# Two-level Strassen MLP: eight weight splits move from the first superblock to the second, and the piece loads of matmul2 keep the program's order

## The chip, the cores and the metric

The kernel runs on one core of a Trainium2 chip. The metric is the device time of one execution in microseconds, as a median over runs. Weights and activations come in as float32 and the result goes out as float32; all matrix products take float16 operands and accumulate in float32.

## The reference

```
x: [8, 1024, 1024]   w1: [1024, 4096]   w2: [4096, 1024]     (float32)
h = x @ w1
h = 0.5 * h * (1 + tanh(sqrt(2 / pi) * (h + 0.044715 * h ** 3)))
out = h @ w2
```

## The kernel before

The 8192 rows of x are taken in eight superblocks of 1024 rows (sb 0 to 7). For each, a first stage computes g = gelu(x @ w1) for all 4096 hidden columns and leaves it in SBUF as four tiles g11, g12, g21 and g22 (two halves of rows by two halves of hidden columns); a second stage computes g @ w2 and stores it.

**Products.** Both stages use a Strassen form: a 2 by 2 block product in seven products, numbered 1 to 7, instead of eight. Products 1, 2 and 3 have a raw block of the weight as operand (block 11, 21, 22), and 5, 6, 7 and 4 have a sum of blocks, which DVE makes. In superblocks 0 and 1 this is done once (one level). From superblock 2 on each of w2's seven operands is itself cut in four quarters, and seven second-level products are taken of it. The second-level operands are again three raw quarters and four sums (5, 6, 7, 4, the tuple `SUMS`). matmul1_late does likewise for part of w1's products, with sums that are called s1, s5, s2, s7 and s3.

**Stages and what they leave in DRAM.** Superblocks 0 and 1 run `matmul1` and `matmul2_made`. While TensorE works there, the operands of the later superblocks are made once and stored in DRAM: w1's in `w1_d`, w2's first-level operands and raw blocks in `w2_d`, and the second-level sums of each w2 operand m in `in_d[m]`. One such second-level sum is called a split here: job `pmn` makes sum n of operand m. It is `make` in `split_jobs`: a buffer, two DVE tensor_tensor instructions, and a 512 KB store issued by POOL (L979). Raw quarters need no split; they are read from `w2_d`.

From superblock 2 on `matmul1_late` and `matmul2` run. matmul1_late works through `PAIR`, an order of small pieces written out by hand, for eight pairs of chunks (`Pair`). Its weights come as eight half-quads, one for each pair (class `StoredHalf`, L284): each loads six pieces of 512 KB, one for each entry of `GROUPS`: operands (1, 5); the sums s1, s5 (in a buffer "mu"); then (2, s2), (7, s7), (3, s3) and (6, 4). The sums s1, s5 of half-quads 1 and 2 are loaded, and those of later ones are made on POOL from operands 1 and 5 (L315, keys k2 to k7 of `PAIR`). Half-quads 0 and 1 of the next superblock are created inside matmul2, when products 7 and 3 begin, and their later pieces are placed in the parts of the g tiles that matmul2 no longer reads (`ROOM`).

matmul2 takes the seven first-level products in the order 4, 1, 2, 5, 6, 7, 3. Each is an object of class `Inner`; `load` fetches its seven second-level pieces on SP's queue, sums from `in_d` (L1034) and raw quarters from `w2_d` (`load_raw`, L1038). The pieces of a product are loaded when the product before it begins, so while product 7 runs, product 3's are asked for. All go in buffers "u", but for the last two steps of product 3: raw quarter 3 goes to a "mu" and sum 4 to the "xi" buffer. Product 4 is begun early: its seven pieces are asked for at the end of matmul1_late.

**Order of jobs in superblocks 0 and 1.** The table `FILL[sb]` gives each slot its jobs. A slot `mq` follows product m's quarter q of the rows; sixteen matmuls of 128x512 make one slot, so it takes 3.46 us of TensorE. The products go 1, 2, 5, 6, 3, 7, 4. Jobs: `g` sums of g, `w` first-level w2 sums, `p` splits, `x` sums of the next x, `q` and `i` sums of w1's next quad and inner sums of x or w1.

**Order of loads.** SP issues nearly all loads. Instructions that go through `load_in_order` (L162) or `tc.keep_in_program_order` keep the order of the program among each other; a plain `nc.sync.dma_start` may be moved by the scheduler that runs when the program is built. In the program as built, SP issues product 3's raw quarter 3 (mu) and sum 4 (xi), and the next superblock's piece (s1, s5) of half-quad 1 (mu), at the end of matmul1_late, ahead of the rest of product 4's pieces.

**Buffers.** Pool `up` has 24 buffers "u" of 512 KB, `mp` 2 "mu", `xip` 1 "xi", `gcp` 4 "gc", `tp` 9 temporaries, and all eight PSUM banks are in use ("ps").

**Engines.** TensorE (PE) multiplies; L497 holds the products of matmul1 and the undivided half products, L712 the second-level parts in matmul1_late, L1082 second-level products in matmul2, L1124 the one-level products of matmul2_made. DVE makes sums (all at L138, helper `tt`) and combines PSUM results; ACT copies (L165) and applies the gelu (L510); POOL makes the inner sums of L315, some adds (L764) and issues the stores to out (L838 and others), the split stores (L979) and the casts of the next x rows (`x_cast`, 256 KB each). SP issues loads and the transposing loads of x (`x_transpose`).

Of the kernel before, what the change touches and what calls it, by code (L numbers as in the profile page):

```python
# [9 lines left out]
DT = mybir.dt.float16  # L10
# [4 lines left out]
P = 128  # L15
# [8 lines left out]
SUMS = tuple(W_SUM)  # L24
# [16 lines left out]
def slots(table):  # L41
# [4 lines left out]
    slots("""10:g60 p15;11:g61 p16;12:g62 p17;13:g63  # L46
    ;20:g50 w50 w51;21:g51 w52;22:w53 g52;23:g53 p14
    ;50:w60 w61;51:w62 w63;52:g30 g31;53:g32 g33
    ;60:w70 p25;61:w71 p26;62:w72 p27;63:w73 p24
    ;30:p35 w40;31:p36 w41;32:p37 w42;33:p34 w43;73:x5;40:x7 x6;41:x3 q5;42:q6 q7 q4  # L50
    ;43:i2 i7 i3 i1 i5""".replace("\n    ", "")),
    slots("""10:g60 w50;11:g61 w51;12:g62 w52;13:g63 w53
    ;20:g50 p55;21:g51 p56;22:g52 p57;23:g53 p54
    ;50:w60 w61;51:w62 w63;52:g30 g31;53:g32 g33
    ;60:p65 w70;61:p66 w71;62:p67 w72;63:p64 w73
    ;30:w40 w41;31:w42 w43;32:p75;33:p76
    ;70:p77 p74;71:x5 p45;72:x7 p46;73:x6 p47
    ;40:p44;41:x3;42:i2;43:i3""".replace("\n    ", "")),
)


# [11 lines left out]
def kernel(  # L73
# [7 lines left out]
    nc = tc.nc  # L81
# [10 lines left out]
    NI = I // P // 2  # L92
    OH = O // 2
# [10 lines left out]
    mp = ctx.enter_context(tc.tile_pool(name="mp", bufs=2))  # L104
# [15 lines left out]
    in_d = {m: dram.tile([P, 4, NI // 2, OH // 2], DT, name=f"in_d{m}") for m in range(1, 8)}  # L120
    w2_d = {
        (k, m): dram.tile([P, 2, 2, HALF], DT, name=f"w2_d{k}_{m}")
        for k in range(2)
        for m in tuple(W_TERM) + SUMS + ("12",)
    }
# [8 lines left out]
    def unit(rows, cols):  # L134
        return up.tile([P, rows, cols], DT, name="u")

    def tt(out, in0, in1, op, pin=False):
        i = nc.vector.tensor_tensor(out=out, in0=in0, in1=in1, op=op)  # L138
        if pin:
            tc.keep_in_program_order(i)  # L140
# [12 lines left out]
    def chunks(t):  # L153
        return t.rearrange("p o (c n) -> p o c n", c=QC)
# [6 lines left out]
    def load_in_order(out, in_, **kw):  # L161
        return tc.keep_in_program_order(nc.sync.dma_start(out=out, in_=in_, **kw))  # L162
# [26 lines left out]
    class MadeQuad:  # L189
# [10 lines left out]
        def load(self):  # L200

            for b, t in self.raw.items():
                k0 = (int(b[0]) - 1) * KH
                halves = t.rearrange("p (h k) n -> p k h n", h=2)
                for k in range(0, KH, 2):
                    cast_in(
                        halves[:, k:k + 2],
                        w1v[int(b[1]) - 1, :, k0 + k:k0 + k + 2, self.q * QW:(self.q + 1) * QW],
                        pool_copy,
                        view=lambda st: st.rearrange("p k (h n) -> p k h n", h=2),  # L210
                    )
# [753 lines left out]
    def split_jobs(m, pieces):  # L965
        t = {}

        def operand(v, h):
            if isinstance(v, int):
                return t[v][:, h * QC:(h + 1) * QC, :]  # L970
            k, b = int(v[0]) - 1, int(v[1]) - 1
            return chunks(pieces()[2 * k + h])[:, b]

        def make(n):
            u, op, v = W_SUM[n]
            t[n] = (mp.tile([P, NI // 2, OH // 2], DT, name="mu") if n in (7, 4) else unit(NI // 2, OH // 2))
            for h in range(2):
                tt(t[n][:, h * QC:(h + 1) * QC, :], operand(u, h), operand(v, h), op, True)
            nc.gpsimd.dma_start(out=in_d[m][:, SUMS.index(n)], in_=t[n])  # L979

        return [lambda n=n: make(n) for n in SUMS]
# [35 lines left out]
    class Inner:  # L1017
# [7 lines left out]
        def load(self, steps=STEPS):  # L1025
            for j in steps:
                if j in self.y:
                    continue
                pool, name = {(3, 3): (mp, "mu"), (3, 4): (xip, "xi")}.get((self.m, j), (up, "u"))
                self.y[j] = pool.tile([P, NI // 2, OH // 2], DT, name=name)  # L1030
                if j in W_TERM:
                    self.load_raw(j)
                else:
                    nc.sync.dma_start(out=self.y[j], in_=in_d[self.m][:, SUMS.index(j)])  # L1034

        def load_raw(self, j):
            k, b = (int(d) - 1 for d in W_TERM[j])
            nc.sync.dma_start(  # L1038
                out=self.y[j].rearrange("p c n -> p (c n)"),
                in_=w2_d[k, self.m][:, b].rearrange("p h n -> p (h n)"),  # L1040
            )

        def make(self, j):
# [219 lines left out]
```

## Time and profile before

| | |
|---|---|
| runs | 1459.35, 1467.58, 1461.14 us |
| median | 1461.14 us |
| profiled execution: its own time | 1462.57 us |
| profiled execution: span | 1460.8 us |
| PE (matmul) | 1450.4 us busy, 99% of the span |
| DVE | 1211.2 us, 83% |
| ACT | 681.1 us, 47% |
| POOL | 620.8 us, 42% |
| granted TensorE clock | 1.0 |
| DMA | 472.72 MB, mean 324 GB/s |
| median of a load u from w_d (SP), issue to landing | 10.2 us (512 KB) |
| median of a load u from in_d (SP) | 10.3 us |
| median of a store out_dram from u (POOL) | 11.1 us |

The profile is that of one execution. Busy time is what an engine worked; its idle time before an instruction is put down to the releaser that came last. In a line of a group or of the timeline, `u<-w_d` is output and input by the program's names, w_d standing for w1_d or w2_d; `x10` is a run of ten instructions; `[1.87 <-DMA u<-w_d]` is 1.87 us of idle time before it, ended by that DMA. Landing is the time from a DMA's issue to its end. Times are microseconds from the start of the span.

### The profile page before, as it was taken

Reading aid. Unit: us, or ns where it says so; the run is one execution under the profiler, and the core shown is the slowest. Engines: PE = TensorE matmul, PEld = TensorE weight load, DVE = VectorE, ACT = ScalarE, POOL = GpSimd, SP = SyncE. Lnnn points to the kernel's source line nnn. Section 1 sums busy time; section 2 is a strip of 40 time slices with the busy share of each in tenths; the row PEclk is TensorE's granted clock in tenths of the full one; section 3 lists DMA queues with packets and bytes.
Section 4 is the critical chain, followed back from the end, with each engine's and each line's share of the span. In section 5 each row is a group of like instructions: output and inputs, shape, how many; then the busy total and the mean of one; then the engine's idle time right before and its main releaser. Section 6 shows DMA issues by size and latency. Waiting matters only on the chain.

```text
span 1460.8 us, 28718 instructions
## 1 busy us (share of the span) xinstructions
PE 1450.4 (99%) x10635; PEld 1039.4 (71%) x10635; DVE 1211.2 (83%) x2029; ACT 681.1 (47%) x1406; POOL 620.8 (42%) x634
## 2 busy tenths in 40 slices
PE   9999999999999999999999999999999999999998
PEld 5444444444467888778877788777887778877887
DVE  5657659748768899889998899988998889988897
ACT  5665116641068611784118831388214872168610
POOL 1442222213359411792128820488005961168411
PEclk9999999999999999999999999999999999999999
DMA  9999999798799999999999999999999989996597
GB/s 322 339 348 383 290 331 358 276 304 259 296 359 272 282 352 366 373 264 337 338 377 370 229 371 336 363 356 225 398 344 362 331 237 389 354 385 231 210 362 265
DMA packets 205709, 472.72 MB, mean 324 GB/s; under 512 B 75648, under 2 KB 80768, under 8 KB 204672
## 3 DMA queue, kind: packets, MB, share of 16 engines
q1 hardware_dynamic: 177632, 373.35, 74.1%
q0 software_dynamic: 27936, 97.53, 22.3%
q8 instruction: 83, 1.36, 0.4%
q14 instruction: 58, 0.48, 0.1%
HBM read 370.15 MB, written 115.34 MB: 332 GB/s over the span
## 4 chain that ended last, share of the span: by engine, by line
PE 87%; DMA 7%; issue 3%; POOL 1%; ACT 0%; SPq 0%; DVE 0%; POOLq 0%; DVEq 0%
PE ps L1082 35%; PE ps L712 23%; PE ps L497 21%; PE ps L1124 7%; DMA gc<-in_w_dram 3%; DMA u<-in_w_dram 2%; DMA w_d<-u 1%; PE ps L430 1%; DMA xb<-in_x_dram 1%; DMA u<-in_d 1%; POOL u L168 0%; POOL out_dram L826 0%; PE ps L407 0%; POOL in_d L979 0%; ACT u L165 0%
## 5 line engine op out<-in xcount | busy, mean ns | idle before, releaser
L165 ACT COPY tmp<-ps 128x512 f32<-128x512 f32 (+1 forms) x536 | 268.8, 540 | 313.3 <-PE ps L497 168.2
L497 PE MATMUL ps<-u 128*128 128x512 f16 x1552 | 363.7, 379 | 3.5 <-DMA u<-w_d 2.7
L1082 PE MATMUL ps<-u,gc 128*128 128x256 f16 x2592 | 290.0, 273 | 0.1
L1082 PEld LDWEIGHTS <-gc 128*128 128x128 f16 x2688 | 263.0, 98 | 30.7 <-issue 0.3
L138 DVE TENSOR_TENSOR tmp<-tmp,ps 128x256 f32<-128x256 f32 (+1 forms) x372 | 199.9, 545 | 87.0 <-PE ps L712 29.8
L497 PEld LDWEIGHTS <-u 128*128 128x128 f16 x1552 | 151.7, 98 | 150.6 <-DMA u<-w_d 3.6
L838 POOL DMA_DIRECT2D out_dram<-u x70 | 63.8, 949 | 443.7 <-DVE u L138 220.3
L712 PEld LDWEIGHTS <-u 128*128 128x128 f16 x2026 | 198.2, 98 | 55.4
L138 DVE TENSOR_TENSOR u<-u 128x2048 f16<-128x2048 f16 (+3 forms) x264 | 204.7, 814 | 33.1 <-DMA w_d<-u 12.6
L165 ACT COPY u<-ps 128x512 f32<-128x512 f32 (+1 forms) x134 | 78.0, 587 | 327.6 <-PE ps L1082 319.3
L1082 PE MATMUL ps<-u,g 128*128 128x256 f16 x1920 | 219.4, 273 | 0.0
L712 PE MATMUL ps<-u 128*128 128x256 f16 x1342 | 216.9, 273 | 0.0
L1082 PEld LDWEIGHTS <-g 128*128 128x128 f16 x2016 | 197.3, 98 | 22.8
L510 ACT ACTIVATE g<-tmp 128x512 f16<-128x512 f32 x282 | 174.0, 640 | 52.2 <-DVE tmp L138 51.2
L138 DVE TENSOR_TENSOR ps<-tmp,ps 128x256 f32<-128x256 f32 x444 | 181.3, 426 | 19.4 <-PE ps L712 12.2
L138 DVE TENSOR_TENSOR u<-u,ps 128x512 f32<-128x512 f32 x216 | 147.2, 683 | 25.9 <-PE ps L1082 16.7
L1124 PE MATMUL ps<-u,g 128*128 128x512 f16 x768 | 166.4, 379 | 0.0
L510 ACT ACTIVATE g<-ps 128x512 f16<-128x512 f32 x230 | 137.8, 600 | 24.8 <-PE ps L712 14.6
L1124 PEld LDWEIGHTS <-g 128*128 128x128 f16 x768 | 75.1, 98 | 90.7
L138 DVE TENSOR_TENSOR tmp<-ps,tmp 128x512 f32<-128x512 f32 x126 | 86.7, 690 | 54.2 <-PE ps L497 42.8
L764 POOL TENSOR_TENSOR tmp<-tmp 128x512 f32<-128x512 f32 x96 | 122.0, 1274 | 20.2 <-DVE tmp L138 13.4
L138 DVE TENSOR_TENSOR gc<-g,gc 128x2048 f16<-128x2048 f16 x78 | 95.1, 1219 | 1.3 <-PE ps L1082 1.3
(70 smaller groups left out, 1506.4 us busy)
## 6 DMA issues: line engine op xcount, KB each, us to landing
u<-w_d SPq DMA_DIRECT2D x347, 512.0 KB, 10.2
u<-in_d SPq DMA_DIRECT2D x162, 512.0 KB, 10.3
out_dram<-u POOLq DMA_DIRECT2D x70, 512.0 KB, 11.1
gc<-in_w_dram SPq DMA_DIRECT2D x48, 512.0 KB, 6.0
g<-w_d SPq DMA_DIRECT2D x45, 512.0 KB, 13.2
w_d<-u POOLq DMA_DIRECT2D x40, 512.0 KB, 7.1
w_d<-u SPq DMA_DIRECT2D x32, 512.0 KB, 8.9
xb<-in_x_dram POOLq DMA_DIRECT2D x56, 256.0 KB, 7.5
```

What stands on the lines that cost most here:

```text
L138: i = nc.vector.tensor_tensor(out=out, in0=in0, in1=in1, op=op)
L165: tc.keep_in_program_order(nc.scalar.copy(out=out, in_=in_))
L430: tc.keep_in_program_order(nc.tensor.matmul(bank[:, cols], lhsT=w[:, k, :], rhs=self.xs.blocks[f"{a}{r}"][:, k, cols], start=r == 1 and k ...
L497: tc.keep_in_program_order(nc.tensor.matmul(bank, lhsT=w, rhs=x, start=first and k == 0, stop=k == n - 1, skip_group_check=not first,))
L510: gelu_last[0] = nc.scalar.activation(out=out, in_=src, func=GELU, scale=scale)
L712: tc.keep_in_program_order(nc.tensor.matmul(out, lhsT=w, rhs=x, start=first and k == 0, stop=k == 1, skip_group_check=not first,))
L764: tc.keep_in_program_order(nc.gpsimd.tensor_tensor(out=t, in0=t, in1=temp("p", m), op=ADD))
L838: return nc.gpsimd.dma_start(out=rows, in_=src, **kw)
L1082: tc.keep_in_program_order(nc.tensor.matmul(bank[:, i * OH // 2:(i + 1) * OH // 2], lhsT=t[:, c, i * P:(i + 1) * P], rhs=self.y[j][:, c, : ...
L1124: tc.keep_in_program_order(nc.tensor.matmul(pair(bank), lhsT=a[:, c, :], rhs=chunks(pieces[c // QC])[:, :, c % QC, :], start=(first and c ...
```

## The change

Eight splits, those of w2's operands 2 and 3 (its raw blocks 21 and 22: p25, p26, p27, p24, p35, p36, p37, p34), leave the slots 60 to 33 of the first superblock's table and enter slots 52 to 41 of the second's. In the first superblock the sums w71 to w73 and w40 to w43 then stand in earlier slots. The moved splits 7 and 4 take "u" buffers instead of "mu". The loads of class `Inner` (L1034 and L1038) go through `load_in_order`. In the program as built, the orders of PE and ACT are as before; on DVE and POOL only the eight splits, their stores and the sums w7n and w4n stand elsewhere. On SP's queue product 3's last two pieces now follow its other five, and the piece (s1, s5) of the next superblock's half-quad 1 follows the first three pieces that go into g22.

```diff
--- before.py
+++ after.py
@@ -46,16 +46,16 @@
     slots("""10:g60 p15;11:g61 p16;12:g62 p17;13:g63
     ;20:g50 w50 w51;21:g51 w52;22:w53 g52;23:g53 p14
     ;50:w60 w61;51:w62 w63;52:g30 g31;53:g32 g33
-    ;60:w70 p25;61:w71 p26;62:w72 p27;63:w73 p24
-    ;30:p35 w40;31:p36 w41;32:p37 w42;33:p34 w43;73:x5;40:x7 x6;41:x3 q5;42:q6 q7 q4
+    ;60:w70 w71;61:w72 w73;62:w40 w41;63:w42 w43
+    ;73:x5;40:x7 x6;41:x3 q5;42:q6 q7 q4
     ;43:i2 i7 i3 i1 i5""".replace("\n    ", "")),
     slots("""10:g60 w50;11:g61 w51;12:g62 w52;13:g63 w53
     ;20:g50 p55;21:g51 p56;22:g52 p57;23:g53 p54
-    ;50:w60 w61;51:w62 w63;52:g30 g31;53:g32 g33
-    ;60:p65 w70;61:p66 w71;62:p67 w72;63:p64 w73
-    ;30:w40 w41;31:w42 w43;32:p75;33:p76
+    ;50:w60 w61;51:w62 w63;52:g30 g31 p25;53:g32 g33 p26
+    ;60:p65 w70 p27;61:p66 w71 p24;62:p67 w72;63:p64 w73
+    ;30:w40 w41;31:w42 w43;32:p75 p35;33:p76 p36
     ;70:p77 p74;71:x5 p45;72:x7 p46;73:x6 p47
-    ;40:p44;41:x3;42:i2;43:i3""".replace("\n    ", "")),
+    ;40:p44 p37;41:x3 p34;42:i2;43:i3""".replace("\n    ", "")),
 )
 
 
@@ -973,7 +973,7 @@
 
         def make(n):
             u, op, v = W_SUM[n]
-            t[n] = (mp.tile([P, NI // 2, OH // 2], DT, name="mu") if n in (7, 4) else unit(NI // 2, OH // 2))
+            t[n] = (mp.tile([P, NI // 2, OH // 2], DT, name="mu") if n in (7, 4) and m not in (2, 3) else unit(NI // 2, OH // 2))
             for h in range(2):
                 tt(t[n][:, h * QC:(h + 1) * QC, :], operand(u, h), operand(v, h), op, True)
             nc.gpsimd.dma_start(out=in_d[m][:, SUMS.index(n)], in_=t[n])
@@ -1031,13 +1031,13 @@
                 if j in W_TERM:
                     self.load_raw(j)
                 else:
-                    nc.sync.dma_start(out=self.y[j], in_=in_d[self.m][:, SUMS.index(j)])
+                    load_in_order(self.y[j], in_d[self.m][:, SUMS.index(j)])
 
         def load_raw(self, j):
             k, b = (int(d) - 1 for d in W_TERM[j])
-            nc.sync.dma_start(
-                out=self.y[j].rearrange("p c n -> p (c n)"),
-                in_=w2_d[k, self.m][:, b].rearrange("p h n -> p (h n)"),
+            load_in_order(
+                self.y[j].rearrange("p c n -> p (c n)"),
+                w2_d[k, self.m][:, b].rearrange("p h n -> p (h n)"),
             )
 
         def make(self, j):
```

## The prediction

> **What bounds the kernel now.** I read the page first, then TensorE's waits, the chain, and around the two places that the change touches the timelines and single DMAs. TensorE is busy throughout:
>
> ```profile
> PE 1450.4 (99%) x10635; PEld 1039.4 (71%) x10635; DVE 1211.2 (83%) x2029; ACT 681.1 (47%) x1406; POOL 620.8 (42%) x634
> ```
>
> The longest of its waits, in all:
>
> ```profile
> PE ps L497 <- DMA u<-w_d: 2.7, 2, 1.9
> ```
>
> So 1460.8 - 1450.4 = 10.4 us of the span are idle PE, the start-up included; only a wait that shows in PE's own idle time can be won back. The chain shows how tight the later superblocks are (start, length, what):
>
> ```profile
> 581.80 2.59 PE ps L497 x12
> ...
> 756.74 2.59 PE ps L497 x12
> ```
>
> That piece opens matmul1_late. It starts at 406.86, 581.80, 756.74, 931.71, 1106.65 and 1281.88: 174.95 us each, but 175.23 for the fifth, which lost 0.28 where product 4's first loads arrived (a chain piece of DMA u<-in_d at 1193.14). All other loss in reach lies between the first two superblocks, in the timeline (idle time before and releaser in brackets):
>
> ```profile
> 201.04 31.97 SPq L198 DMA_DIRECT2D u<-w_d  x10
> ...
> 211.33 1.90 PE L497 MATMUL ps<-u 128*128 128x512 f16 x8 [1.87 <-DMA u<-w_d]
> ...
> 214.02 10.53 PE L497 MATMUL ps<-u 128*128 128x512 f16 x48 [0.79 <-DMA u<-w_d]
> ...
> 225.40 9.87 PE L497 MATMUL ps<-u 128*128 128x512 f16 x45 [0.84 <-DVE tmp L138]
> ```
>
> 1.87 + 0.79 + 0.84 = 3.5 us. SP issues the second superblock's w1 quad only at 201.04, behind 16 transposing loads that ran from 167.92 to 197.34 while eight split stores and x stores shared the DMA engines.
>
> **Part 1, splits leave the first superblock.** Eight splits (p25 to p34) go. Each is two DVE instructions (1.29 us the pair), one POOL issue (0.54) and a 512 KB store: 10.3 us of DVE, which waited there anyway, and 4 MB of stores between 168 and 195. In the changed program's order the quad's four buffers come from sums of product 5 and from staging tiles, free long before, no longer from split tiles that wait for their stores. In later superblocks a transposing load takes 1.25 us of SP, so 16 take 20, not 29.4; the quad's loads start some 9 us earlier, against 3.5 of stall. I take the whole 3.5 as gained (bounds 0 and 3.5).
>
> **Part 2, splits enter the second superblock.** The same 10.3 us of DVE. p25 to p24 stand before 368.98, where DVE sat idle 9.62 us: hidden, with some 4 us left. p35 to p34 add 5.2 us from 376 on; gaps of 1.6, 1.5 and 6.1 us (until 409.98) take them. The new tile of a split may wait for an earlier split's store (4 to 10 us to landing there); behind it on DVE stand x3 and the inner sums. x3 is read by PE at 413.17 and was ready at 398.45; the inner sum of product 2 is read at 409.50 and was ready at 399.91, so 9.6 us of cover. Of POOL's eight issues and stores, those of p37 and p34 stand after the last store of a mu tile. Cost 0; if the cover is gone, up to 3 us (a rival below).
>
> **Part 3, the pinned loads.** The old order hoists three loads per superblock, product 3's last two (mu, xi) and the next superblock's mu (sums s1, s5 of half-quad 1), to the end of matmul1_late, some 90 us before use:
>
> ```profile
> 655.74 2.22 SPq L1038 DMA_DIRECT2D mu<-w_d  x1
> ...
> 663.70 0.49 SPq L284 DMA_DIRECT2D mu<-w_d  x1
> 667.92 0.32 SPq L1034 DMA_DIRECT2D xi<-in_d  x1
> ```
>
> They delay product 4's loads by three landings of 1.28 us, and xi's wait for its buffer (to 667.92) holds the queue. Those loads land 0.04 to 2.9 us before use; the new order gives them 4 us more. Since PE barely waited there, that wins 0.28 us in all.
>
> In the new order mu and xi follow product 3's other loads, and the third comes after three g loads: all three stand in the stretch where matmul2 ends. There the DMA engines are full, and POOL's stores of products 7 and 3 share them:
>
> ```profile
> L838 POOL DMA_DIRECT2D out_dram<-u x6: 725/794/1227, 745.8 to 757.8; - x6
> ...
> DMA to landing us min/median/max: 10.8/14.8/16.7
> ```
>
> While stores are queued, SP's loads land every 2.5 us (754.21, 756.83, 759.59, 762.14, 764.64, 767.12, 769.62, then 774.10 with two x casts between); before and after it is 1.28 (775.96, 777.17, 778.47). SP's own issue does not limit this: it issues when the load eight before has landed. Watch the sixth DMA behind the first three g loads, half-quad 1's (6,4) operand, issued at 746.97, with those behind it:
>
> ```profile
> 746.97 0.32 SPq L284 DMA_DIRECT2D u<-w_d  x1
> 755.02 0.32 SPq L284 DMA_DIRECT2D mu<-w_d  x1
> 755.38 19.05 SPq L284 DMA_DIRECT2D u<-w_d  x10
> ```
>
> Its own landing (min, median, max of this one DMA), and its first reader:
>
> ```profile
> DMA to landing us min/median/max: 17.7/17.7/17.7
> ```
> ```profile
> 771.98 1.03 PE L497 MATMUL ps<-u 128*128 128x512 f16 x4
> ```
>
> It lands at 764.64 and is read at 771.98: 7.3 us of cover. With three more loads ahead and the stores unchanged it gets the landing of the DMA three places behind, issued at 755.86, 18.2 us to landing: 774.10. PE would wait 774.10 - 771.98 = 2.1 us. The same reading at the five ends of a matmul2 that has a successor:
>
> - end at 581.80: read 597.03, new landing 599.55, wait 2.5
> - 756.74: 771.98, 774.10, 2.1
> - 931.71: 946.95, 949.18, 2.2
> - 1106.65: 1121.89, 1125.31, 3.4
> - 1281.88: 1297.12, 1297.65, 0.5
>
> Sum 10.7 us. The other loads of the stretch keep a little cover in this shift (product 3's own mu and xi 1.3 to 3.4 and 0.3 to 3.6 us; g loads down to -0.3), and those after 1121.89 gain what PE has already waited. Bounds: one landing of 1.28 either way at each place gives 5 to 17. The lower end at no sharing is a rival.
>
> The row that decides is the landing every 2.5 us beside stores. [...]
>
> **Sum** against the profiled execution (1462.57, span 1460.8): 1462.57 - 3.5 - 0.3 + 10.7 = 1469.5, +0.47%. The median of the runs shown (1461.14) is 1.4 below that execution; +0.47% on it is 1468.
>
> **Rivals.**
>
> *Gain alone.* The three loads cost 3 x 1.28 = 3.8 us of DMA time, less than the 4.6 to 7.3 us of cover at the (6,4) operand. If they displace stores rather than loads, nothing waits and 3.8 is won: 1461.14 - 3.8 = 1457.3. For it: no wait of PE there now. Against: the 2.5 us spacing holds at all five ends, whether five or eight loads are outstanding.
>
> *POOL's chain on top, slower.* POOL's first sum of half-quad 3 (L315) starts at 779.87, 0.16 after its load landed at 779.71. Behind it on POOL stands the second add of L764, for which a Gelu on ACT waits; that Gelu ran 1.36 us after the add, and the bank freed behind it was reused 0.94 us later: 2.3 us of cover. Three places on, the load lands at 785.90, 6.2 later; less 2.1 that PE already lost and 2.3 of cover, 1.8 more per end. About 2 us at five ends: 1468 + 10 = 1478. It decides once that load is over 4.4 us late. Against it: 3.6 of the 6.2 are two x casts, started by POOL behind PE's own progress, so they move back too; then it is near 3.8.
>
> *The clock.* The granted clock is 1.0 in all 40 slices, and idle times up to 1.87 did not lower it; the first seven matmuls took 3.17 us, 0.45 each against 0.216 later. A wait of 3.4 us, longer than any in this trace, could bring that back: ten matmuls at 0.23 more are 2.3 us per end, at one to four ends 1470 to 1477. [...]
>
> *Second superblock.* SP's order now has two mu loads behind each other at 400.65, the second waiting for the last mu store (landed 402.35, later by what DVE adds). If that holds half-quad 1's loads (cover 7.3 to 11.5 us) over 7 us, some 3 us are added: 1471.
>
> **How the numbers follow.** Forecast 0.52, its own range 1462 to 1474; gain alone 0.20; POOL's chain 0.13; clock 0.07; second superblock 0.08. 0.5% (7.3 us) is about what a measurement of this kernel can tell from no change. More than 7.3 won is out of reach, since 3.8 is all there is: 0.03, out of gain alone, for the runs' scatter. The forecast stands at the edge: 0.24 of it slower, the rest same. Slower: 0.24 + 0.13 + 0.06 + 0.06 = 0.49; same 0.48. Range: from gain alone (1457) to POOL's chain (1478), with 2 us at each end since the two medians scatter: 1455 to 1480.
>
> **What would show it.** Right: no idle PE near 201 to 226; PE waits of 2 to 3 us on DMA u<-w_d about 15 us after each matmul1_late starts, and periods near 177; product 4's loads landing 4 us or more ahead. Wrong: periods still 174.95 (gain alone); waits on ACT or POOL near 24 us (POOL's chain); matmuls 0.43 us apart (clock); PE idle between 407 and 430 (second superblock); or the 3.5 us at 211 still there.

## The result and the profile after

The changed kernel takes 1476.43 us (median of six runs, 1472.05 to 1478.50) against 1460.99 us for the kernel before (six runs). The ratio is 1.0101, with a 95% interval of 1.0081 to 1.0121: it is slower by about 15 us. The profiled execution took 1477.74 us with a span of 1476.0.

The page's line for TensorE, and then the list of its waits (total, times, longest):

```profile
PE 1454.5 (99%) x10635; PEld 1038.6 (70%) x10635; DVE 1210.7 (82%) x2029; ACT 680.9 (46%) x1406; POOL 620.0 (42%) x634
```
```profile
PE ps L497 <- DMA u<-w_d: 6.5, 3, 3.3
PE ps L497 <- ACT tmp L165: 5.5, 2, 2.8
```

Idle PE has grown from 10.4 us to 1476.0 - 1454.5 = 21.5. That is 11.1 of the 15.2 us by which the span grew; the other 4.1 are *busy* PE. The waits on DMA were there before (2.7 us), though not in these places; those on ACT are new.

Both kernels issue the same 10635 matmuls in the same order. So the start of each matmul in one trace can be set against the same matmul in the other, and what the difference grows by in a stretch is what that stretch cost. An end is the stretch where a matmul2 gives way to the next matmul1_late; the five are numbered in order of time. The (6,4) operand is that of half-quad 1, the load that the prediction follows. In us against the profiled execution before:

| stretch | after | of it PE's wait at the (6,4) operand or a g load | wait behind POOL | half-rate clock |
|---|---|---|---|---|
| start-up, to 30 us | -0.72 | | | |
| first to second superblock, 200 to 235 | -4.01 | | | |
| second superblock to 560 | +0.37 | 0.36 | | |
| end 1 (start 581.80 before) | +4.60 | 0 | 2.93 | 1.66 |
| end 2 (756.74) | +5.63 | 1.04 | 2.95 | 1.66 |
| end 3 (931.71) | +5.16 | 3.26 | 0 | 1.70 |
| end 4 (1106.65) | +3.44 | 3.43 | 0 | 0 |
| near 1201 | -0.29 | | | |
| end 5 (1281.88) | +1.00 | 0.99 | 0 | 0 |

The sum is +15.2, the whole growth of the span. The rest of end 3 is a step of 0.21 ahead of its wait. The start-up's 0.7 has nothing to do with the change: all later kernels but two show -0.7 to -1.0 there against this one execution.

The gain is where it was looked for. SP issues the second superblock's w1 quad at 193.75 us, 7.3 us earlier than before (some 9 were forecast). In the timeline the second superblock now begins without a wait, where before three pieces stood with 1.87, 0.79 and 0.84 us of idle time:

```profile
206.63 2.11 PE L1124 MATMUL ps<-u,g 128*128 128x512 f16 x9
208.57 14.62 PE L497 MATMUL ps<-u 128*128 128x512 f16 x67
```

The loss at end 2 shows all three mechanisms. SP's queue issues the (6,4) operand at 751.57, the answer on that one DMA gives 21.6 us to landing (17.7 before), and the matmul that reads it starts when it lands, at 773.25:

```profile
751.57 0.32 SPq L284 DMA_DIRECT2D u<-w_d  x1
```
```profile
DMA to landing us min/median/max: 21.6/21.6/21.6
```
```profile
773.25 1.04 PE L497 MATMUL ps<-u 128*128 128x512 f16 x4 [0.88 <-ACT g L510]
```

(751.57 + 21.6 = 773.2. The trace names ACT as releaser, but the 0.05 us between landing and start says that it is the load.) Some 12 us on, POOL's sum of half-quad 3 (L315) waits for its load, and the add of L764 stands behind it. An ACT copy out of PSUM waits for that add: it writes a temporary (`tmp<-ps`), so it needs a free buffer and not the add's result; by the code the add is the last reader of one. The PE waits for the bank that the copy empties. POOL before, and then POOL, ACT and PE after:

```profile
777.97 1.28 POOL L764 TENSOR_TENSOR tmp<-tmp 128x512 f32<-128x512 f32 x1
779.87 1.15 POOL L315 TENSOR_TENSOR mu<-u 128x512 f16<-128x512 f16 x1 [0.62 <-PE ps L712]
780.98 1.27 POOL L764 TENSOR_TENSOR tmp<-tmp 128x512 f32<-128x512 f32 x1
```

```profile
779.26 1.28 POOL L764 TENSOR_TENSOR tmp<-tmp 128x512 f32<-128x512 f32 x1
785.77 1.15 POOL L315 TENSOR_TENSOR mu<-u 128x512 f16<-128x512 f16 x1 [5.23 <-DMA u<-w_d]
786.88 1.26 POOL L764 TENSOR_TENSOR tmp<-tmp 128x512 f32<-128x512 f32 x1
```
```profile
788.18 0.59 ACT L165 COPY tmp<-ps 128x512 f32<-128x512 f32 x1 [4.37 <-POOL tmp L764]
```
```profile
788.81 1.04 PE L497 MATMUL ps<-u 128*128 128x512 f16 x4 [2.78 <-ACT tmp L165]
```

Then come 4 us in which the PE is busy and does half its work. The windows view (window, its length, busy time and instructions of PE, PEld, DVE, ACT and POOL, granted clock, DMA share, GB/s) for the wait and for what follows it:

```profile
785.50:788.80 3.30, 0.54 (x5) 0.33 (x4) 0.01 (x1) 0.62 (x2) 3.03 (x3) 1.00 1.03 423
788.80:792.90 4.10, 4.09 (x16) 2.03 (x16) 2.72 (x6) 3.58 (x7) 4.10 (x4) 0.61 1.02 415
```

At end 1 a window inside such a spell reads 0.50 (in the last section). At that rate a granted clock of 0.61 over 4.1 us is half rate for 3.2 us; over a 5.1 us window it reads 0.67 at ends 1, 2 and 3 alike, 3.4 us at half rate, so 1.7 us of work lost each time. Three such spells cost 5.0 us. That busy PE grew by 4.1 only is because other stretches had less of it, the start-up above all (25.40 us for its 185 matmuls, 27.23 before).

### The profile page after: what moved, and what is told of

It reads as the page before. It is cut to its first block, busy times and chain, and to the rows that moved or that the text cites. A ratio compares the mean times of both kernels' runs of the same rounds, so it can differ in the third digit from the quotient of the medians.

```text
span 1476.0 us, 28744 instructions
## 1 busy us (share of the span) xinstructions
PE 1454.5 (99%) x10635; PEld 1038.6 (70%) x10635; DVE 1210.7 (82%) x2029; ACT 680.9 (46%) x1406; POOL 620.0 (42%) x634
## 4 chain that ended last, share of the span: by engine, by line
PE 77%; DMA 22%; POOL 0%; SPq 0%; issue 0%; DVE 0%; ACT 0%; POOLq 0%; DVEq 0%; ACTq 0%
PE ps L497 22%; PE ps L1082 21%; PE ps L712 19%; PE ps L1124 13%; DMA u<-w_d 8%; DMA g<-w_d 6%; DMA xi<-in_d 3%; DMA out_dram<-u 2%; DMA mu<-w_d 2%; PE ps L430 1%; DMA gc<-in_w_dram 1%; DMA u<-in_d 0%; SPq L162 0%; POOL tmp L764 0%; POOL mu L315 0%
## 5 line engine op out<-in xcount | busy, mean ns | idle before, releaser
L497 PE MATMUL ps<-u 128*128 128x512 f16 x1552 | 366.5, 381 | 13.1 <-DMA u<-w_d 6.5
L497 PEld LDWEIGHTS <-u 128*128 128x128 f16 x1552 | 152.1, 98 | 162.4 <-DMA u<-w_d 9.0
L712 PEld LDWEIGHTS <-u 128*128 128x128 f16 x2026 | 199.0, 98 | 56.7 <-issue 1.5
L138 DVE TENSOR_TENSOR u<-u 128x512 f32<-128x512 f32 (+3 forms) x272 | 208.7, 807 | 33.4 <-DMA w_d<-u 12.6
L712 PE MATMUL ps<-u 128*128 128x256 f16 x1342 | 217.8, 273 | 0.0
L764 POOL TENSOR_TENSOR tmp<-tmp 128x512 f32<-128x512 f32 x96 | 122.0, 1273 | 19.9 <-DVE tmp L138 11.2
L712 PE MATMUL ps<-gc,mu 128*128 128x256 f16 x504 | 96.2, 273 | 0.0
```

The source lines that it names most:

```text
L497: tc.keep_in_program_order(nc.tensor.matmul(bank, lhsT=w, rhs=x, start=first and k == 0, stop=k == n - 1, skip_group_check=not first,))
L712: tc.keep_in_program_order(nc.tensor.matmul(out, lhsT=w, rhs=x, start=first and k == 0, stop=k == 1, skip_group_check=not first,))
L764: tc.keep_in_program_order(nc.gpsimd.tensor_tensor(out=t, in0=t, in1=temp("p", m), op=ADD))
```

## The experiments

All comparisons are with the kernel before, run on the same chip (1459.3 to 1460.6 us).

**The change taken in two.** One kernel moves the splits and leaves the loads unpinned, the other pins the loads and leaves the splits.

```
e1_splits:  FILL and mu/unit as changed;  L1034, L1038: nc.sync.dma_start as before
e2_pins:    FILL and mu/unit as before;   L1034, L1038: load_in_order
```

> Only the splits move; the loads of matmul2 stay unpinned, so that mu, xi and the next superblock's mu go out at the end of matmul1_late as before. Theory A (the loss sits in the late place of the three loads): the 4.0 us gained at 208 to 221 stay and the five ends keep their 174.95 us periods: about 1457, 4 under before. Rival B (TensorE reaching the first end 4.4 us earlier, beside loads that do not move with it, is what starves that end): a wait of about 3 us at 27 us after the first end and a half-rate clock behind it, so 1461, no change.

> Only the loads of matmul2 are pinned; the splits stay in the first superblock. Theory A: waits of 3 us or more at all ends but the last, with the half-rate clock behind some: before plus 15 to 20, so 1476 to 1481. Rival B: the first end, now reached 4.4 us later, loses nothing, and the rest as in the changed kernel: before plus 11 to 15, so 1472 to 1476.

Measured: e1_splits 1460.2 (ratio 0.9994, 0.9978 to 1.0011); e2_pins 1475.22 (1.0080, 1.0052 to 1.0109). The loss comes with the pinned loads; with the splits alone none is left. Theory A was right about the ends in e1_splits (its profile loses nothing at any of the five) and about the 4.01 us won at 200 to 235; rival B's wait is not in it. But the median didn't fall by 4: in this execution 2.87 us were lost between 400 and 560 (1.4 of it in a wait for a load at 418.8), and its other runs spread from 1457.6 to 1464.5. In e2_pins the ends cost 2.4, 6.2, 2.4, 1.6 and 0. Its trace shows another thing: with the splits in their old place the wait at the start of the second superblock was 8.0 us in that execution, against 1.87 in the profile before and 3.3 in e11_k_late_only below. The old place costs a varying amount.

```profile
217.26 15.02 PE L497 MATMUL ps<-u 128*128 128x512 f16 x58 [8.01 <-DMA u<-w_d]
```

**Only the POOL chain.** In `PAIR`, k7 moves from ahead of the add v1 to behind it.

```
-... c5 x15 k7 m22' z23' v1' m16 ...
+... c5 x15 m22' z23' v1' k7 m16 ...
```

> The changed kernel with POOL's order altered alone: k7, the first sum of a half-quad that POOL makes from a load, stands behind the add v1 instead of ahead of it. Theory A (the waits at 608 and 789 are the Gelu behind POOL's add, held by a sum whose load is late): these two waits (2.8 us each) go and with them the half-rate clock behind them (1.6 each): 1476.4 - 9 = 1467. Rival (the late loads hold TensorE directly a little later): the time comes back as a wait on the sums or on a DMA: 1473 to 1477.

Measured: 1467.46 (1.0035, 1.0018 to 1.0051), the figure of theory A. Its profile shows no wait on ACT at L497 any more:

```profile
PE ps L497 <- DMA u<-w_d: 8.8, 5, 3.0
```

The sum itself still starts only when its load is there, at 605.84 by POOL's timeline, but both adds now run ahead of it:

```profile
599.12 2.51 POOL L764 TENSOR_TENSOR tmp<-tmp 128x512 f32<-128x512 f32 x2
605.84 1.16 POOL L315 TENSOR_TENSOR mu<-u 128x512 f16<-128x512 f16 x1 [4.21 <-PE ps L712]
```

The size came out for a mixed reason. Ends 1 to 5 cost 0.57, 4.85, 3.15, 1.98 and 1.25: the POOL waits are gone at ends 1 and 2, and at end 2 a DMA wait of 3.2 with a half-rate clock behind it took the place, while the clock did not fall at end 3 this time.

**Which of the three late loads.** In e6_xi_early the loads of sums are unpinned again; xi then goes out early, and the raw quarter (mu) and the next superblock's mu stay late. (In that kernel's trace SP issues this xi at 668.86 and the pinned raw quarter at 737.45, though the program asks for the raw quarter first: a load that is not pinned can still move past pinned ones.)

```
-                    load_in_order(self.y[j], in_d[self.m][:, SUMS.index(j)])
+                    nc.sync.dma_start(out=self.y[j], in_=in_d[self.m][:, SUMS.index(j)])
```

> The changed kernel with the loads of sums unpinned: xi goes out early again, the raw quarter in mu and the next superblock's mu stay late, so two loads of three are late. Theory A (each late load costs a landing of 2.5 us against covers of 4.6 to 7.3 us at the (6,4) operand): it lands 2.5 us earlier than in the changed kernel, the waits at ends 3 and 4 shrink from 3.3 to under 1 and the rest go, no half-rate clock: 1457 to 1463. Rival (every late load costs its share): two thirds of the 19.5 us lost at the ends, 1457 + 13 = 1470.

Measured: 1476.95 (1.0103, 1.0079 to 1.0127). Both theories missed: taking one load of three back won nothing. Ends 1 to 5 cost 4.70, 4.45, 5.51, 5.57 and 0.40, by waits for the (6,4) operand at ends 1 and 3, a wait of 1.1 us for a later load at end 2, waits behind POOL at ends 2, 3 and 4, and a fallen clock at ends 1 and 4. So the late loads do not add up, and the next three kernels place them one by one, all with the splits moved and the loads pinned.

Abridged:

```
e4_all_early, in matmul2 ahead of products[4].load():
+        products[3].load((3,))
+        made = mp.tile(...)    # the next superblock's mu, handed to StoredHalf(1)
+        load_in_order(made, w1_d[0, ("s1", "s5")][:, 1])
+        products[3].load((4,))
e7_next_mu_early: only the two lines of made
e8_next_mu_late:  products[3].load((3, 4)) there; the next mu loaded in order where StoredHalf(1) is made
```

> Splits moved and loads pinned as in the changed kernel, but the three loads are asked for by the program ahead of product 4's pieces, so that the pin keeps them early. Theory A (their place costs, not the pin): as with the splits alone, 1458 to 1461. Rival (the pin itself, its order between the other loads, costs): 1470 or more.

> The changed kernel, with the next superblock's mu (sums s1, s5 of half-quad 1) early and product 3's raw quarter and xi late. Theory P (place: product 3's two land ahead of the stores, 1.3 to 2.5 us apart, and only the load among the stores displaces what PE waits for): no wait over 1 us at the ends, 1458 to 1463. Rival N (number: two loads of 512 KB late are as much as with xi early, wherever they stand): 1470 to 1477.

> The reverse: product 3's raw quarter and xi early, the next superblock's mu late, behind three loads of g22. Theory P: it displaces the (6,4) operand and half-quad 3's load by 2.5 to 5 us: some waits of 1 to 3 us remain, 1466 to 1476. Rival N: one late load costs 2.5 us against covers of 4.6 to 7.3, so nothing: 1458 to 1462.

Measured:

| late | kernel | us | ratio, 95% interval |
|---|---|---|---|
| none | e4_all_early | 1459.88 | 1.0008 (0.9997 to 1.0018) |
| raw quarter 3, xi | e7_next_mu_early | 1468.10 | 1.0060 (1.0037 to 1.0082) |
| next mu | e8_next_mu_late | 1471.98 | 1.0087 (1.0070 to 1.0104) |
| raw quarter 3, next mu | e6_xi_early | 1476.95 | 1.0103 (1.0079 to 1.0127) |
| all three | after | 1476.43 | 1.0101 (1.0081 to 1.0121) |

The pin as such costs nothing; the place costs. Theory P is right on e8 and wrong on e7, where product 3's two loads also cost; rival N is wrong on e8, where a single late load of 512 KB costs 12.7 us of median. That was the surprise: at the (6,4) operand one landing of 2.5 us had 4.6 to 7.3 us of cover (the time from landing to first reader). The waits of e8_next_mu_late tell where it went:

```profile
PE ps L497 <- ACT tmp L165: 6.6, 3, 2.7
PE ps L497 <- DMA u<-w_d: 2.3, 2, 1.3
```

6.6 us are the POOL chain, at ends 2, 3 and 4; of the waits on DMA 1.3 us stand at end 1, the rest near 418. In e7's profile the same chain costs 2.7 and 3.2 us at ends 2 and 3, with 1.2 us at a (6,4) load of half-quad 2 ahead of the one and a half-rate clock behind the other. POOL's first sum of half-quad 3 was waiting for its load in the kernel before already (0.16 us between landing and start), so every microsecond that this load comes later is one that POOL stands. Only the slack behind the add covers it, which by the changed kernel's ends 1 and 2 is 1.9 and 1.7 us (the load 4.8 and 4.6 us late, the PE's wait 2.93 and 2.95).

**One late load with the chain loosened.** If that reading is right, e8's single late load must become harmless when k7 stands behind v1.

> The kernel with the next superblock's mu alone late, and POOL's k7 behind v1. Theory T (POOL's first sum is the tightest reader after an end, 1.8 to 2.3 us of cover; the (6,4) operand has 4.6 to 7.3): the waits of 2.9 us on ACT at the ends go and one of 1 to 1.5 us at the first end stays: 1458 to 1462. Rival (one late load is too much for the (6,4) operand or another load as well): 1466 or more.

Measured: 1460.29 (1.0000, 0.9989 to 1.0011). The 12.7 us are gone with a change in POOL's order alone. Its list of waits has no wait of L497 on ACT or on a load any more, and 1.1 us in three waits of L712 on ACT in their place:

```profile
PE ps L712 <- ACT tmp L165: 1.1, 3, 0.6
```

The 1.3 us that theory T left at the first end did not come either.

**Where the 2.5 us between landings comes from.**

```
-        products[7].rows = out("22", accum_op=ADD)
+        if end:
+            products[7].rows = out("22", accum_op=ADD)
...
-        else:
-            products[3].rows = out("12")
...
-                    if b[1] == "2":
+                    if b[1] == "2" and end:
```

> The changed kernel without POOL's output stores of product 7, of product 3 and of the sums with product 7, in all superblocks but the last: this leaves that part of the output unwritten. Theory A (the loads around an end land 2.5 us apart because these stores take half of the DMA engines): they land 1.3 us apart, the (6,4) operand 5 us or more before its read, no waits at the ends: 1455 to 1461. Rival (SP's issue or buffers that come free late set the spacing): waits of 3 us stay, 1470 or more.

Measured: 1457.97 (0.9988, 0.9973 to 1.0003). With all three loads late but those stores left out, the loads around end 2 land 1.28 us apart, once 1.49 (755.19, 756.68, 757.96, 759.24, 760.52) and the five ends cost nothing. The (6,4) operand takes 11.3 us from issue to landing, where the changed kernel has 21.6:

```profile
DMA to landing us min/median/max: 11.3/11.3/11.3
```

It lands at 757.96 and is read at 767.53. So the sharing with POOL's stores is what makes a late load dear. Without the stores buffers may also come free sooner, but that did little for this operand: against the PE's own progress it was issued only 0.25 us earlier than in the changed kernel (746.64 against 751.57, where the PE was 4.68 us ahead).

**A kernel faster than both.** The splits moved, the loads as before, k7 behind v1; and k7 behind v1 alone as its control.

> The splits alone moved, the loads early and unpinned, and POOL's k7 behind v1. Theory T: the 4.8 us gained at 208 to 221 are in part lost in some executions at the POOL chain, as in the profile with all three early; with the chain loosened 1456 to 1458, 0.2 to 0.3% under before. Rival (they are lost elsewhere, at 418 and in the third superblock): 1459 to 1461.

> The kernel before with k7 behind v1 alone. In its profile no wait stands at the POOL chain, so by both theories no change in the profiled time; if some executions of the kernel before do wait there, the median falls by up to 1 us: 1459 to 1461.

Measured: e10_splits_k_late 1458.01 (0.9981, 0.9967 to 0.9995); e11_k_late_only 1459.26 (1.0002, 0.9990 to 1.0014). The first beats the kernel before by 0.05 to 0.33%. In its profile the 4.01 us won at 200 to 235 last to the end, the five ends cost nothing, and the PE is idle for under 7 us in all:

```profile
span 1456.1 us, 28722 instructions
...
PE 1449.2 (100%) x10635; PEld 1038.9 (71%) x10635; DVE 1211.0 (83%) x2029; ACT 680.8 (47%) x1406; POOL 620.6 (43%) x634
```

Its eleven runs lie between 1457.4 and 1459.4; those of the kernel before reach from 1457.6 to 1469.7. This fits a splits' move that mostly takes away a loss which comes in some executions; only the profiled ones show where it stands. The control's profiled execution had one of these: 3.3 us of wait at 212.64 in the timeline, and 1.6 more to the clock.

```profile
212.64 13.87 PE L497 MATMUL ps<-u 128*128 128x512 f16 x56 [3.27 <-DMA u<-w_d]
```

In e4_all_early's profile end 1 cost 4.24 us, a wait of 2.4 us behind POOL and the clock after it, although all three loads were early: the chain has so little cover that an execution can fall into it even so. In e10 the sum stands behind the add, and its profile shows no such wait.

## Why the prediction was right or wrong

The direction, slower, was right; the size was not: +7 was forecast, +15 came. The sum held the five waits of the PE on a load and put POOL's chain and the clock at nothing; these two came to 10.9 us.

- **Splits out of the first superblock: right.** 3.5 forecast; 4.01 in the profiles that move them, 3.85 in e3_k_late's. What it left out is that the loss taken away varies between executions, so the medians show less of it.
- **Splits into the second superblock: nearly right.** Forecast 0, 0.37 in the profile after. Between 400 and 560 it is 0.3 to 2.9 across the kernels that move them and 0 in the two that do not. The most, in e1_splits, is a wait of 1.4 for the load that is read near 418 and two of 0.5 near 500. The rival of that place asked for 3.
- **0.3 us won at product 4's first loads: wrong cause.** The 0.29 at 1201 is gone in e11_k_late_only too, where SP's order is as before. It was chance in one execution.
- **Five waits on the (6,4) operand, 10.7 us: right in kind, 8.7 in size.** Forecast 2.5, 2.1, 2.2, 3.4, 0.5; measured 0, 1.04, 3.26, 3.43 and 0.99 (at end 5 0.65 at a g load, the rest there). Against TensorE's own delay the operand of ends 2 to 5 came 8.3, 10.5, 8.6 and 4.9 us later, where the shift of three landings said 9.5, 9.6, 8.7 and 5.1. At end 1 it came 4.6 later instead of 9.0, since there a pair of x casts landed behind it and not ahead of it.
- **POOL's chain: the step that failed.** The prediction had found it, with the right sum and add, and set it aside as a rival at 0.13, because the casts "move back too". It gave 2.3 us of cover, by a Gelu on ACT; the copy ahead of that Gelu is what waits, and the cover was 1.9 and 1.7. The sum's load came 4.8 and 4.6 us late at ends 1 and 2 where the PE had not yet waited for it, which left 2.93 and 2.95 us of wait. It was also taken as coming on top of the five waits at every end. In fact the two share: where the (6,4) operand had already cost 3.3 us (ends 3 and 4), PE and POOL reached the sum later: at end 3 it did not wait for its load, at end 4 for 1.77 us, which cost the PE nothing. The cover at the (6,4) operand was the wrong one to build the sum on: at 4.6 to 7.3 us it was not the smallest after an end, the chain's of under 2 us was.
- **The clock: a rival that should have been a term.** It was given 0.07, and only for a wait of 3.4 us. It fell at three ends of five, after waits of 2.8 and 3.1 us, for 5.0 us in all. That it takes 3.4 us, and that ten slow matmuls at 2.3 us per end follow, was the author's estimate and shown by no run; the spells cost 1.66 to 1.70 each.
- **Gain alone: refuted** by e2_pins. **The stores' share of the DMA engines: borne out** by e9_no_stores, 1.28 us between most landings without these stores and 2.5 with them. By what rule a DMA engine shares itself between loads and stores, no run shows; that the stores keep their part against three more loads, on which the 10.7 rested, was the author's estimate. In the changed kernel the loads around end 2 still land 2.5 us apart (762.14, 764.64, 767.14, 769.64), as they did before the change.

By the table the terms are: -0.7 -4.0 +0.4 -0.3, then 8.7 of DMA waits with 0.2 beside them, 5.9 behind POOL and 5.0 to the clock, which is +15.2.

## What to carry to other kernels

When a transfer is moved later, look for the reader with the least cover after it on *any* engine, not for the nearest reader on the bound engine: an instruction that already waits for its load and has others queued behind it is the first to pass the delay on. Put such an instruction behind the work that does not need the load. And where a change brings longer waits on a TensorE that is otherwise always busy, count a half-rate clock after them as a possible cost of its own: here it followed 11 of 17 waits of 2.4 to 3.3 us, at about 1.7 us each.

## What the runs showed of the hardware that was not expected

The clock fell after shorter waits than the 3.4 us that the prediction counted with. The traces of the kernels above hold 17 waits of the PE of 2.4 to 3.3 us, each begun at a granted clock of 1.00. After 11 of them, the shortest of 2.40 us (e4_all_early), the granted clock over the next 5 us read 0.67; after 6 it stayed at 1.00, once behind a wait of 3.26 us (the changed kernel's end 4). After nine waits of 1.2 to 2.3 us it stayed at 1.00, as it did behind the 1.87 us at 211.33 in the kernel before. So length alone doesn't decide, and what else does, these runs do not show.

The half-rate spells of the changed kernel begin at 608.78, 789.68 and 956.94 and last 3.41 us each; 0.67 over 5.1 us, as behind all 11 waits, is 3.4 us at half rate too. The windows view at end 1 of the changed kernel (2.76 us idle, then half rate, then full) and at end 4 (3.22 us idle, no fall):

```profile
605.36:608.78 3.42, 0.66 (x4) 0.29 (x3) 0.59 (x1) 1.21 (x3) 3.42 (x4) 1.00 1.03 417
608.78:612.19 3.41, 3.41 (x13) 1.67 (x11) 2.13 (x6) 2.99 (x6) 3.41 (x3) 0.50 1.02 417
612.19:615.60 3.41, 3.41 (x28) 2.61 (x27) 2.47 (x6) 1.78 (x5) 3.39 (x6) 1.00 1.03 411
```
```profile
1132.90:1136.30 3.40, 0.18 (x2) 0.00 (x0) 0.75 (x2) 1.01 (x2) 1.72 (x2) 1.00 0.85 312
1136.30:1140.00 3.70, 3.65 (x23) 2.27 (x24) 2.51 (x6) 2.14 (x4) 0.00 (x0) 1.00 1.03 422
```

The work behind the 8.0 us wait of e2_pins was slower for longer: the 58 matmuls there took 15.02 us, 0.259 each, against 14.62 us for 67, 0.218 each, at the same place in the changed kernel. That is 2.4 us more, where a spell at an end cost 1.7.
